# A hybrid decoder layer on one core: logits of head pairs as 64-row products in two-bank tiles, values projected 512 columns at once, q and k split once, stick products on GpSimd

## The chip, the cores and the metric

One of the eight cores of a Trainium2 chip runs the kernel. The metric is the device time of one execution in microseconds (us). The kernel before takes 709.08 us, the median of three runs (707.87 to 709.63).

## What is computed

One decoder layer and a final norm, for 512 tokens of width 1024, all in float32:

```python
h = h + W_o [ stick-breaking heads || differential heads ](RMSNorm(h) W_in)
h = h + W_down( gelu(g) * u ),  [g, u] = causal_dwconv3( RMSNorm(h) W_up )
h = h + sigmoid(RMSNorm(h) W_pg) * (p W_pp)
```

Eight stick-breaking heads of dimension 64 weigh token s for token t by beta_ts times the product of (1 - beta_tj) over s < j < t, where beta is the sigmoid of the scaled logits and s < t. Four differential heads have two maps of dimension 64 each: the weights are softmax(Q1 K1' + b1) - lambda softmax(Q2 K2' + b2), the values are 128 wide, and each head's output is normalized. The FFN is 2816 wide.

## The kernel before

All matrix products keep float32 accuracy by splitting each operand into a high and a low part of a reduced type (float32r); `mm3` then makes three products: high x high, low x high, high x low. `split_w` makes the parts of a weight, 128x1024 at a time: the cast of the high part on ScalarE (ACT), the subtraction for the low part on VectorE (DVE).

**The stages.** x is loaded, transposed and scaled into `xg` (eight tiles, hidden dimension on partitions). `proj_qk` projects q and k of a pair of heads (128 columns each, 24 products of 512 columns each for q and for k). There are eight such pairs: four of stick heads and four of the two maps of a differential head. `proj_v` projects values, 256 columns at a time, in four calls of 96 products. `sb_logits` and `sb_attn` do a stick pair: logits in five banks with the causal mask added by a product, two sigmoids on ACT, a scan on DVE for the running product of (1 - beta), a multiplication by beta on DVE (line L418), transposes on TensorE (PE), the split of the weights (L432, L433), the weighted sums. `diff_probs` does a differential head's logits and softmax, by blocks of 128 tokens: a reduction from PSUM on DVE (L479), an exponential on ACT (L483), the two maps combined (L488, L489). `diff_out` does the transposes (L503), the split, the weighted sums, and the norm: squares on ACT, their sums on PE (L516), a power on GpSimd (POOL, L106), and a broadcast on PE (`bcast_row`, L116). The output projection comes in two halves: the first sums over the stick heads (mix tiles 0 to 3), the second over the differential heads (mix 4 to 7) and feeds `residual`, whose squares POOL adds up (L539). The FFN starts from about 264 us.

**The operands of the logits.** The contraction is only 64 deep, so `proj_qk` stacks the high and the low part of q on the 128 partitions (`st`), and holds the high part of k on both halves (`dh`) and the low part on both halves (`dl`): two products of 128 rows give all four terms for one head. The copy into the other half is made by POOL (L341), 32 copies of 64x512.

**PSUM** has eight banks: pool `psA` has two one-bank tiles `mm` for projections and six one-bank tiles `z` for all else. `slot` gives the work tiles, 128x512 each.

**What sets the order.** The program is written in one sequence; a scheduler then orders each engine's instructions by its own estimate of when they can start and by priorities. Within an engine the order is then fixed and each instruction waits for what it needs. The table `fill` puts weight loads and projections of later pairs beside a stick pair's attention. The second value projection stands in pair 1, the third in pair 3, the fourth among the differential heads. After the attention the same PSUM pool goes on, as a ring of all eight tiles:

```python
ring = itertools.cycle([psm, psm, psz, psz, psz, psz, psz, psz])
self.psm = lambda: next(ring)()
```

Of the kernel before, what the change touches and what calls it, by code (L numbers as in the profile page):

```python
# [35 lines left out]
SLOTS = {"w": 7, "h": 6, "l": 6, "strip": 2, "qkt": 2, "o": 2}  # L36
# [4 lines left out]
class Kern:  # L41
# [24 lines left out]
    def slot(self, s, tag="w"):  # L66
        return self.work.tile([P, T], F32, tag=tag, name=self.nm(s), bufs=SLOTS[tag])

# [242 lines left out]
    def proj_qk(self, sp, stacked):  # L311

# [4 lines left out]
        halves = [slice(0, HD), slice(HD, P)]  # L317
        for i in range(2):
# [7 lines left out]
            if i == stacked:  # L326
                st = self.qk.tile([P, 2, T], F32R, tag="st", name=self.nm("st"))
                for h in range(2):
                    nc.scalar.copy(st[halves[h], h, :], t[halves[h], :])
                    nc.vector.tensor_sub(st[halves[1 - h], h, :], t[halves[h], :], st[halves[h], h, :].bitcast(F32))  # L330
                res.append(st)
            else:
                dh = self.qk.tile([P, 2, T], F32R, tag="dh", name=self.nm("dh"))
                dl = self.qk.tile([P, 2, T], F32R, tag="dl", name=self.nm("dl"))
                for h in range(2):
                    o = halves[h]
                    nc.scalar.copy(dh[o, h, :], t[o, :])  # L337
                    nc.vector.tensor_sub(dl[o, h, :], t[o, :], dh[o, h, :].bitcast(F32))  # L338
# [3 lines left out]
                res.append((dh, dl))  # L342
        return res

    def prep_v(self, off):
        raw = self.load_w([(0, self.a["w_in"][0][:, off : off + 2 * P])], KT, 2 * P)
        return [self.split_w(raw[:, i * 4 : (i + 1) * 4, :]) for i in range(2)]

    def proj_v(self, sp, stacked):

        nc = self.nc
        v = self.vp.tile([P, NB, 4 * P], F32R, tag="v", name=self.nm("v"))
        for tb in range(NB):
            ps = self.psv()
            for k in range(KT):
                xs = tuple(x[:, tb * P : (tb + 1) * P] for x in self.xg[k])
                self.mm3(ps[:, : 2 * P], xs, tuple(x[:, k % 4, :] for x in sp[k // 4]), k == 0, k == KT - 1)
            r = self.rstd1[:, tb : tb + 1]
            if stacked:
                oh, ol = (v[:, tb, :].rearrange("p (h d) -> p h d", d=HD)[:, i::2, :] for i in range(2))  # L360
                pv = ps[:, : 2 * P].rearrange("p (h d) -> p h d", d=HD)
            else:
                oh, ol = v[:, tb, : 2 * P], v[:, tb, 2 * P :]
                pv = ps[:, : 2 * P]
# [6 lines left out]
    def sb_logits(self, q, k):  # L371
        nc = self.nc

        banks = [[(h, 3, 0)] for h in range(2)] + [[(h, 2, 0), (h, 0, 384)] for h in range(2)] + [[(0, 1, 0), (1, 1, 256)]]
        z = []
        for parts in banks:
            ps = self.psz()
            z.append(ps)
            first = True
            for h, tb, col in parts:  # L380
                n = (tb + 1) * P
                for x in range(2):
                    nc.tensor.matmul(
                        ps[:, col : col + n], lhsT=q[:, h, tb * P : (tb + 1) * P], rhs=k[x][:, h, :n],
                        start=first, stop=False, skip_group_check=True,
                    )
                    first = False
# [444 lines left out]
```

## Time and profile before

| what | value |
|---|---|
| median of three runs | 709.08 us (707.87 to 709.63) |
| the profiled execution, its own time | 708.74 us |
| span of its trace | 707.0 us |
| TensorE (PE) busy | 681.5 us, 96% |
| VectorE (DVE) busy | 465.4 us, 66% |
| ScalarE (ACT) busy | 333.3 us, 47% |
| GpSimd (POOL) busy | 93.0 us, 13% |

The profile is that of one execution. Busy time is that of instructions that compute; a product's time in it is longer than the place it takes, since products overlap, so how fast products follow each other is read from their starts. The granted clock is TensorE's, as a share of full speed. The releaser of a wait is the instruction that ended it. Time outside of the span is 1.7 us.

### The profile page before, as it was taken

The numbers are of one execution on the slowest core, as the hardware profiler recorded it, in microseconds if no ns is written. First come the engines' busy times: TensorE is split into PE (matmuls) and PEld (weight loads), VectorE is DVE, ScalarE is ACT, GpSimd is POOL, SyncE is SP. The second block draws the span as 40 slices with busy tenths as digits, with TensorE's granted clock in tenths as the row PEclk, the third lists the DMA queues.
The fourth block names the chain that finished last, engine by engine and source line by source line (L and its number), as shares of the span: only waits on it lengthen the run. The fifth ranks groups of instructions, "written<-read, shape, count | busy, mean of one in ns | idle before, by whom it ended". The sixth has DMA issues, their size and how long they took to land. (4 is left out here: it accounts for less than half of the span.)

```text
span 707.0 us, 8645 instructions
## 1 busy us (share of the span) xinstructions
PE 681.5 (96%) x3363; PEld 573.0 (81%) x3363; DVE 465.4 (66%) x719; ACT 333.3 (47%) x535; POOL 93.0 (13%) x84
## 2 busy tenths in 40 slices
PE   6998999899999998999999999999999999999995
PEld 5887888788988876888888888888888878888885
DVE  6777979978686648597777777677734241516444
ACT  5555655667674435455444444444423131417422
POOL 2233034304221006000000000000000010102001
PEclk9999999999999999999999999999999999999998
DMA  8763231142351103333322233321423222327002
GB/s 270 245 244 94 60 109 44 28 119 90 90 208 62 60 0 98 91 110 120 119 74 87 79 120 119 100 79 59 131 93 105 66 98 90 104 62 265 1 28 92
DMA packets 69840, 72.72 MB, mean 103 GB/s; under 512 B 2357, under 2 KB 60926, under 8 KB 69799
## 3 DMA queue, kind: packets, MB, share of 16 engines
q1 hardware_dynamic: 66464, 65.80, 29.1%
q10 hardware_dynamic: 2695, 4.27, 1.6%
q0 software_dynamic: 640, 2.10, 0.7%
q8 instruction: 26, 0.43, 0.3%
q14 instruction: 15, 0.12, 0.1%
HBM read 67.95 MB, written 6.84 MB: 106 GB/s over the span
## 5 line engine op out<-in xcount | busy, mean ns | idle before, releaser
L99 DVE TENSOR_TENSOR wlo<-wraw,whi 128x1024 fp32r<-128x1024 f32 (+1 forms) x104 | 127.6, 1229 | 87.2 <-ACT whi L98 86.0
L98 ACT CAST whi<-wraw 128x1024 fp32r<-128x1024 f32 (+1 forms) x104 | 107.4, 1034 | 148.8 <-PE z L80 85.7
L539 POOL TENSOR_TENSOR sqacc<-sqacc,sq 128x512 f32<-128x512 f32 x14 | 22.4, 1603 | 364.2 <-issue 259.1
L79 PE MATMUL mm<-xgh,whi 128*128 128x512 f32 x128 | 50.5, 395 | 1.4 <-ACT whi L98 1.4
L80 PE MATMUL mm<-xgl,whi 128*128 128x512 f32 x128 | 50.3, 394 | 0.0
L81 PE MATMUL mm<-xgh,wlo 128*128 128x512 f32 x128 | 50.2, 392 | 0.0
L341 POOL TENSOR_SCALAR dh<-dh 64x512 fp32r<-64x512 f32 x16 | 28.2, 1759 | 115.2 <-ACT dh L337 103.8
L691 DVE TENSOR_TENSOR vpad<-z,rb 128x512 f32<-128x512 f32 x34 | 23.2, 687 | 26.8 <-PE z L81 26.7
L693 ACT ACTIVATE y<-vpad,par,par 128x512 f32<-128x512 f32 x44 | 35.7, 814 | 3.2 <-DVE vpad L691 3.0
L79 PE MATMUL mm<-whi,xgh 128*128 128x256 f32 x96 | 28.7, 299 | 6.0 <-DVE v L367 5.9
L695 DVE SCALAR_TENSOR_TENSOR y<-vpad,par,y 128x512 f32<-128x512 f32 x44 | 32.9, 751 | 1.3
L694 DVE SCALAR_TENSOR_TENSOR y<-vpad,par,y 128x512 f32<-128x512 f32 x44 | 32.7, 745 | 0.0
L697 ACT ACTIVATE y<-y 128x512 f32<-128x512 f32 x22 | 13.9, 630 | 34.9 <-DVE y L695 34.8
L79 PEld LDWEIGHTS mm<-xgh,whi 128*128 128x128 f32 x128 | 24.2, 189 | 6.4 <-ACT whi L98 1.8
L80 PE MATMUL mm<-wlo,xgh 128*128 128x256 f32 x96 | 28.6, 298 | 0.0
L81 PE MATMUL mm<-whi,xgl 128*128 128x256 f32 x96 | 28.6, 298 | 0.0
L81 PEld LDWEIGHTS mm<-xgh,wlo 128*128 128x128 f32 x128 | 24.1, 188 | 4.8
L80 PEld LDWEIGHTS mm<-xgl,whi 128*128 128x128 f32 x128 | 24.2, 189 | 4.5
L417 DVE TENSOR_TENSOR_SCAN cum<-cum,fresh 128x512 f32<-128x512 f32 x20 | 25.2, 1270 | 1.4 <-ACT cum L408 1.1
L79 PEld LDWEIGHTS mm<-whi,xgh 128*128 128x128 f32 x96 | 19.5, 203 | 6.9 <-DVE v L367 6.3
L341 POOL TENSOR_SCALAR dl<-dl 64x512 fp32r<-64x512 f32 x16 | 24.9, 1558 | 1.5 <-DVE dl L338 0.3
L483 ACT ACTIVATE pr<-pr,nmx 128x512 f32<-128x512 f32 (+3 forms) x32 | 17.7, 556 | 10.9 <-DVE nmx L479 10.7
(673 smaller groups left out, 1925.0 us busy)
## 6 DMA issues: line engine op xcount, KB each, us to landing
wraw<-in_w_up SPq DMA_DIRECT2D x22, 1024.0 KB, 5.1
wraw<-in_w_in SPq DMA_DIRECT2D x16, 512.0 KB, 7.1
wraw<-in_w_down SPq DMA_DIRECT2D x8, 1024.0 KB, 4.9
wraw<-in_w_in SPq DMA_DIRECT2D x5, 1024.0 KB, 5.1
wraw<-in_w_o SPq DMA_DIRECT2D x4, 1024.0 KB, 5.0
wraw<-in_w_ple_gate SPq DMA_DIRECT2D x4, 1024.0 KB, 5.7
wraw<-in_w_down SPq DMA_DIRECT2D x4, 768.0 KB, 4.2
sk<-sk ACTq DMA_DIRECT2D x1, 2560.0 KB
```

Source lines behind the costliest of these rows:

```text
L79: nc.tensor.matmul(ps, lhsT=l[0], rhs=r[0], start=start, stop=False, **kw)
L80: nc.tensor.matmul(ps, lhsT=l[0], rhs=r[1], start=False, stop=False, **kw)
L81: nc.tensor.matmul(ps, lhsT=l[1], rhs=r[0], start=False, stop=stop, **kw)
L98: nc.scalar.copy(hi, raw)
L99: nc.vector.tensor_sub(lo, raw, hi.bitcast(F32))
L341: nc.gpsimd.tensor_scalar(x[halves[1 - h], h, :], x[halves[h], h, :].bitcast(F32), 1.0, None, op0=ALU.mult)
L417: nc.vector.tensor_tensor_scan(back, back, fresh, 1.0, op0=ALU.mult, op1=ALU.max)
L539: nc.gpsimd.tensor_add(sqacc, sqacc, sq)
L691: nc.vector.tensor_mul(u[:, 2 : T + 2], ps, rb2)
L693: nc.scalar.activation(y, u[:, 2 : T + 2], AF.Identity, scale=self.cw(2, ch), bias=self.g("cb", ch))
L694: nc.vector.scalar_tensor_tensor(y, u[:, 1 : T + 1], self.cw(1, ch), y, op0=ALU.mult, op1=ALU.add)
L695: nc.vector.scalar_tensor_tensor(y, u[:, 0:T], self.cw(0, ch), y, op0=ALU.mult, op1=ALU.add)
```

## The change

- `psA` has three two-bank tiles `z` in place of six of one bank, and the work tiles of `slot` are two banks wide and half as many.
- `proj_qk` splits q and k once, 128x512 each: high part by ACT, low part by DVE. Nothing is stacked or copied to another half.
- `logits`, new, serves both kinds of heads. A pair's two heads lie on partitions 0 to 63 and 64 to 127. For each block of 128 tokens three products of 64 rows (high x low, low x high, high x high) are made for each head, the two heads by turns, each into its own bank of a two-bank tile: 24 products a pair, where there were 16 of 128 rows.
- `proj_v` projects 512 columns in one call of 96 products into four banks: the stick values ahead of pair 0, the differential ones after head 0's logits.
- `sb_attn` works on three two-bank tiles: sigmoids up to 1024 wide, scans 512 wide, the multiplication by beta on GpSimd, up to 1024 wide. `diff_out` evicts 1024 and 256 columns in place of four pieces.
- `fill` is gone. `psA` is closed after the attention, and the second half of the output projection and all that follows uses a new pool of eight one-bank tiles.

```diff
-SLOTS = {"w": 7, "h": 6, "l": 6, "strip": 2, "qkt": 2, "o": 2}
+SLOTS = {"w": 4, "h": 3, "l": 3, "strip": 2, "qkt": 2, "o": 2}
+WIDE = ("w", "h", "l")
...
+        shape = [P, 2, T] if tag in WIDE else [P, T]
+        return self.work.tile(shape, F32, tag=tag, name=self.nm(s), bufs=SLOTS[tag])
...
-                for x in (dh, dl):
+            o = self.qk.tile([P, 2, T], F32R, tag=tag, name=self.nm(tag))
+            nc.scalar.copy(o[:, 0, :], t)
+            nc.vector.tensor_sub(o[:, 1, :], t, o[:, 0, :].bitcast(F32))
+            res.append(o)
+        return res
+
+    def logits(self, q, k):
...
+        z = [self.psz() for _ in range(3)]
+        where = {3: (0, 0), 2: (1, 0), 0: (1, 3 * P), 1: (2, 0)}
+        with self.tc.high_priority(2000):
+            for tb in (3, 2, 0, 1):
+                b, col = where[tb]
+                n = (tb + 1) * P
+                for i, (x, y) in enumerate(((0, 1), (1, 0), (0, 0))):
                     for h in range(2):
-                        nc.gpsimd.tensor_scalar(x[halves[1 - h], h, :], x[halves[h], h, :].bitcast(F32), 1.0, None, op0=ALU.mult)
...
+                        o = slice(h * HD, (h + 1) * HD)
+                        nc.tensor.matmul(
+                            z[b][:, h, col : col + n], lhsT=q[o, x, tb * P : (tb + 1) * P], rhs=k[o, y, :n],
+                            start=i == 0 and tb != 0, stop=i == 2 and tb != 2, skip_group_check=True,
+                        )
+        return z, where
+
+    def proj_v(self, off, stacked):
...
+        v = self.vp.tile([P, NB, 2 * T], F32R, tag="v", name=self.nm("v"))
+        pss = [z[:, i, :] for z in (self.psz(), self.psz()) for i in range(2)]
+        for k0 in range(0, KT, 4):
+            raw = self.load_w([(0, self.a["w_in"][0][k0 * P : (k0 + 4) * P, off : off + T])], 4, T)
+            for i in range(2):
+                wh, wl = self.split_w(raw[:, 2 * i : 2 * i + 2, :])
+                for tb in range(NB):
+                    for j in range(2):
+                        k = k0 + 2 * i + j
+                        xs = tuple(x[:, tb * P : (tb + 1) * P] for x in self.xg[k])
+                        self.mm3(pss[tb], xs, (wh[:, j, :], wl[:, j, :]), k == 0, k == KT - 1)
...
-            nc.vector.tensor_mul(beta, beta, c[:, 1 : T + 1])
...
+            for c0 in range(off, 2 * T, T):
+                back = c[:, c0 : c0 + T][:, ::-1]
+                r0 = (3 - g) * P
+                fresh = self.fresh[:, r0 : r0 + T] if g else self.fresh[:, 0:1].to_broadcast([P, T])
+                nc.vector.tensor_tensor_scan(back, back, fresh, 1.0, op0=ALU.mult, op1=ALU.max)
+            nc.gpsimd.tensor_mul(beta, beta, c[:, off + 1 : 2 * T + 1])
...
-        self.psz = lambda: psA.tile([P, T], F32, tag="z", name=self.nm("z"), bufs=6)
+        self.psz = lambda: psA.tile([P, 2, T], F32, tag="z", name=self.nm("z"), bufs=3)
...
-        fill = {0: [(wv, mv, 0), (wq, mq, 1)], 1: [(wv, mv, 1), (wq, mq, 2)], 2: [(wq, mq, 3)], 3: [(wq, mq, 4), (wv, mv, 2)]}
-        mv(0)
+        v = self.proj_v(2 * SBW, True)
         for pair in range(4):
             lg = self.sb_logits(*qk[pair])
-            for w, _, i in fill[pair]:
-                w(i)
-            self.sb_attn(pair, lg, v[pair // 2])
...
+            wq(pair + 1)
+            self.sb_attn(pair, lg, v)
+            mq(pair + 1)
...
         pr[0] = self.diff_probs(0, *qk[4])
         mq(5)
         wq(6)
-        wv(3)
+        v = self.proj_v(5 * SBW, False)
...
-        mv(3)
...
         self.close("work", "vp", "qk")
-        psm, psz = self.psm, self.psz
-        ring = itertools.cycle([psm, psm, psz, psz, psz, psz, psz, psz])
-        self.psm = lambda: next(ring)()
+        self.close("psA")
+        psB = self.open("psB", space=PSUM)
+        self.psm = lambda: psB.tile([P, T], F32, tag="mm", name=self.nm("mm"), bufs=8)
```

**How the order moves: PE at stick pair 3.** Before, at the transposes of pair 3 (L430, from `beta`), with `mm` the projection of q of the second differential head:

```order
L79 MATMUL mm_1668<-xgh_148,whi_1585 128x512
L80 MATMUL mm_1668<-xgl_149,whi_1585 128x512
L430 MATMUL z_1334<-ident,beta_1329 128x128
L430 MATMUL z_1334<-ident,beta_1319 128x128
L430 MATMUL z_1334<-ident,beta_1309 128x128 x2
L430 MATMUL z_1343<-ident,beta_1329 128x128
L430 MATMUL z_1343<-ident,beta_1324 128x128
L430 MATMUL z_1343<-ident,beta_1314 128x128 x2
```

Behind the last transpose sixteen more products of that `mm` tile and five of the next follow before the first weighted sum (L442). Now, from the third logits tile of pair 3 (`z_1065`) over its masks (L386) to the transposes (L432, into `z_1124`):

```order
L445 MATMUL z_980<-awl_976,v_396 128x256
L445 MATMUL z_980<-awh_953,v_396 128x128
L445 MATMUL z_980<-awl_954,v_396 128x128
L346 MATMUL z_1065<-k_1060,q_1030 128x256 x6
L386 MATMUL z_1065<-maskR,identR 128x128 x2
L432 MATMUL z_1124<-ident,beta_1119 128x128
L432 MATMUL z_1124<-ident,beta_1113 128x128
L432 MATMUL z_1124<-ident,beta_1107 128x128 x2
```

No projection stands between the masks and the transposes any more; the nine products nearest to them (L81 to L83 into an `mm` tile) stand just ahead of the eight weighted sums of pair 2 that these rows end. Further on, head 0's last logits (`z_1265`) and then the wide value projection (`z_1402`):

```order
L445 MATMUL z_1160<-awl_1156,v_396 128x256
L445 MATMUL z_1160<-awh_1133,v_396 128x128
L445 MATMUL z_1160<-awl_1134,v_396 128x128
L346 MATMUL z_1265<-k_1240,q_1210 128x256 x6
L81 MATMUL z_1402<-whi_1406,xgh_123 128x512
L82 MATMUL z_1402<-wlo_1407,xgh_123 128x512
L83 MATMUL z_1402<-whi_1406,xgl_124 128x512
L81 MATMUL z_1402<-whi_1406,xgh_135 128x512
```

Before, the values of the first two differential heads were 256 columns wide, in `mm` tiles, and stood ahead of pair 3's transposes; now those of all four come behind head 0's logits.

**PE at the output projection and differential head 3.** Before, around head 3's logits (L477), with `mm_2614` and `mm_2628` of the first half (mix 0 to 3):

```order
L477 MATMUL z_2361<-dl_2295,st_2262 128x384
L477 MATMUL z_2372<-dh_2294,st_2262 128x256
L477 MATMUL z_2372<-dl_2295,st_2262 128x256
L80 MATMUL mm_2614<-mix3l,whi_2610 128x512
L81 MATMUL mm_2614<-mix3h,wlo_2611 128x512
L79 MATMUL mm_2628<-mix0h,whi_2610 128x512
L80 MATMUL mm_2628<-mix0l,whi_2610 128x512
L81 MATMUL mm_2628<-mix0h,wlo_2611 128x512
```

and some 60 rows later the second half (mix 4 and on) ahead of head 2's weighted sums (`z_2432`):

```order
L81 MATMUL mm_2660<-mix3h,wlo_2643 128x512
L79 MATMUL mm_2703<-mix4h,whi_2699 128x512
L80 MATMUL mm_2703<-mix4l,whi_2699 128x512
L81 MATMUL mm_2703<-mix4h,wlo_2700 128x512
L79 MATMUL mm_2703<-mix5h,whi_2699 128x512
L80 MATMUL mm_2703<-mix5l,whi_2699 128x512
L81 MATMUL mm_2703<-mix5h,wlo_2700 128x512
L79 MATMUL z_2432<-dwh_2404,v_2126 128x512
```

Now head 3's logits (L346, `z_1965` and `z_1966`) stand behind the last product of the first half (`mm_2270`, six rows above these) and inside head 1's weighted sums (`z_1831`):

```order
L81 MATMUL z_1831<-dwh_1820,v_1401 128x384
L82 MATMUL z_1831<-dwl_1821,v_1401 128x384
L83 MATMUL z_1831<-dwh_1820,v_1401 128x384
L81 MATMUL z_1831<-dwh_1827,v_1401 128x256
L346 MATMUL z_1965<-k_1928,q_1898 128x512 x6
L346 MATMUL z_1966<-k_1928,q_1898 128x384 x6
L346 MATMUL z_1966<-k_1928,q_1898 128x128 x6
L82 MATMUL z_1831<-dwl_1828,v_1401 128x256
```

and the second half's first product (`mm_2317`) behind the last broadcast (L118) of head 3's norm:

```order
L118 MATMUL z_2112<-identR,bch_2137 128x128
L118 MATMUL z_2112<-identR,bcl_2138 128x128
L81 MATMUL mm_2317<-mix4h,whi_2313 128x512
L82 MATMUL mm_2317<-mix4l,whi_2313 128x512
L83 MATMUL mm_2317<-mix4h,wlo_2314 128x512
L81 MATMUL mm_2317<-mix5h,whi_2313 128x512
L82 MATMUL mm_2317<-mix5l,whi_2313 128x512
L83 MATMUL mm_2317<-mix5h,wlo_2314 128x512
```

The rows between `z_1965` and `mm_2317` are the transposes, weighted sums, norms and logits of the differential heads; no row of the projection is among them.

## Rows read from the trace of the kernel before

**Rows 1.** The page, parts 1 and 2: busy time of the engines, granted TensorE clock.

```profile
PE 681.5 (96%) x3363; PEld 573.0 (81%) x3363; DVE 465.4 (66%) x719; ACT 333.3 (47%) x535; POOL 93.0 (13%) x84
...
PEclk9999999999999999999999999999999999999998
```

**Rows 2.** PE's waits: engine, line waited for, us in total, times, longest.

```profile
PE mm L79 <- DVE v L367: 5.9, 2, 3.3
```

**Rows 3.** Timeline of PE: start, us, instruction, idle before and its releaser.

```profile
59.13 0.28 PE L81 MATMUL mm<-whi,xgl 128*128 128x256 f32 x1
62.73 0.39 PE L79 MATMUL mm<-whi,xgh 128*128 128x256 f32 x1 [3.32 <-DVE v L367]
```

**Rows 4.** Stretches: length, busy us of PE, PEld, DVE, ACT, POOL, clock, DMA.

```profile
64.20:67.70 3.50, 3.50 (x19) 3.50 (x19) 0.00 (x0) 0.00 (x0) 0.00 (x0) 0.51 0.02 5
139.30:142.80 3.50, 3.50 (x19) 3.50 (x19) 1.78 (x3) 1.03 (x1) 0.00 (x0) 0.51 0.00 0
270.00:275.00 5.00, 3.67 (x16) 2.33 (x14) 5.00 (x5) 3.08 (x5) 3.97 (x4) 1.00 0.00 0
275.00:280.00 5.00, 3.75 (x16) 2.66 (x15) 5.00 (x5) 1.24 (x2) 2.60 (x2) 1.00 0.01 3
```

**Rows 5.** Timeline of PE, differential head 3.

```profile
222.43 0.48 PE L477 MATMUL z<-dh,st 128*128 128x512 f32 x1
222.74 0.39 PE L477 MATMUL z<-dl,st 128*128 128x512 f32 x1
222.97 0.39 PE L477 MATMUL z<-dh,st 128*128 128x512 f32 x1
...
224.13 0.28 PE L477 MATMUL z<-dh,st 128*128 128x256 f32 x1
224.25 0.28 PE L477 MATMUL z<-dl,st 128*128 128x256 f32 x1
...
241.38 1.29 PE L503 MATMUL z<-ident,pr 128*128 128x128 f32 x10
243.34 0.49 PE L79 MATMUL z<-dwh,v 128*128 128x512 f32 x1 [0.67 <-ACT dwh L505]
...
254.53 0.27 PE L116 MATMUL z<-identR,bcl 128*128 128x128 f32 x1
```

**Rows 6.** Groups of DVE, ACT, POOL to 300 us: count, busy us, mean ns, idle before.

```profile
L99 DVE TENSOR_TENSOR wlo<-wraw,whi 128x1024 fp32r<-128x1024 f32 x41 | 52.6, 1288 | 17.5 <-ACT whi L98 17.3
L417 DVE TENSOR_TENSOR_SCAN cum<-cum,fresh 128x512 f32<-128x512 f32 x20 | 25.2, 1270 | 1.4 <-ACT cum L408 1.1
L338 DVE TENSOR_TENSOR dl<-qkt,dh 64x512 fp32r<-64x512 f32 x16 | 13.0, 813 | 0.2
L479 DVE CUSTOM_DVE_ANT_0 pr<-z,strip 128x512 f32<-128x512 f32 x8 | 5.4, 690 | 0.9 <-PE z L477 0.8
L489 DVE SCALAR_TENSOR_TENSOR pr<-pr,rsm,pr 128x512 f32<-128x512 f32 x4 | 3.0, 748 | 0.5 <-ACT pr L488 0.5
...
L98 ACT CAST whi<-wraw 128x1024 fp32r<-128x1024 f32 x41 | 42.8, 1046 | 42.1 <-PE mm L80 13.3 <-PE z L80 8.1 <-DMA wraw<-in_w_in 7.1
L337 ACT CAST dh<-qkt 64x512 fp32r<-64x512 f32 x16 | 9.9, 616 | 2.6 <-DVE qkt L325 2.4
L483 ACT ACTIVATION_READ_ACCUMULATOR pr<-pr,nmx 128x1 f32 x32 | 6.0, 188 | 0.0
L483 ACT ACTIVATE pr<-pr,nmx 128x512 f32<-128x512 f32 x8 | 5.7, 719 | 10.3 <-DVE nmx L479 10.3
L538 ACT ACTIVATE sq<-hT 128x512 f32<-128x512 f32 x7 | 4.2, 618 | 0.3 <-POOL sqacc L539 0.3
...
L341 POOL TENSOR_SCALAR dh<-dh 64x512 fp32r<-64x512 f32 x16 | 28.2, 1759 | 115.2 <-ACT dh L337 103.8 <-issue 10.7
L539 POOL TENSOR_TENSOR sqacc<-sqacc,sq 128x512 f32<-128x512 f32 x7 | 11.3, 1620 | 17.9 <-ACT sq L538 17.6
L106 POOL TENSOR_TENSOR rcd<-nrv,mhalf 128x4 f32<-128x4 f32 x4 | 4.1, 1023 | 46.2 <-DVE nrv L105 31.8 <-PE z L477 14.4
```

More of the change, by code (lines that the diff above doesn't have):

```diff
@@ L309, in prep_qk, with proj_qk @@
         return [self.split_w(raw[:, :, i * P : (i + 1) * P]) for i in range(2)]
-    def proj_qk(self, sp, stacked):
+    def proj_qk(self, sp):
         nc = self.nc
         res = []
-        halves = [slice(0, HD), slice(HD, P)]
-        for i in range(2):
+        for i, tag in enumerate("qk"):
             wh, wl = sp[i]
@@ L353, in proj_v @@
         for tb in range(NB):
[L354 to L357, printed above, removed]
             r = self.rstd1[:, tb : tb + 1]
@@ L372, in sb_logits @@
         nc = self.nc
[L374 to L387, printed above, removed]
-            diag = [col // P + tb for _, tb, col in parts]
-            step = diag[1] - diag[0] if len(diag) == 2 else 1
-            nc.tensor.matmul(
-                ps.rearrange("p (a b) -> p a b", b=P)[:, diag[0] :: step, :], lhsT=self.identR,
-                rhs=self.maskR.unsqueeze(1).to_broadcast([P, len(diag), P]), start=False, stop=True, skip_group_check=True,
-            )
@@ L395, in sb_logits, with sb_attn @@
-        return banks, z
-    def sb_attn(self, pair, logits, v):
+        z, _ = self.logits(q, k)
+        for b, (d, nd) in enumerate(((3, 1), (2, 2), (1, 1))):
+            for h in range(2):
+                nc.tensor.matmul(
+                    z[b][:, h, :].rearrange("p (a b) -> p a b", b=P)[:, d : d + nd, :], lhsT=self.identR,
+                    rhs=self.maskR.unsqueeze(1).to_broadcast([P, nd, P]), start=False, stop=True, skip_group_check=True,
+                )
+        return z
+    def sb_attn(self, pair, z, v):
@@ L400, in sb_attn @@
         nc = self.nc
[L401 to L402 removed]
         at = {}
[L404 to L405 removed]
+        for g in range(3):
+            w = 2 * P if g == 2 else T
+            n = 2 * w
+            beta = self.slot("beta").rearrange("p a b -> p (a b)")[:, :n]
             c = self.cum[self.ncum % len(self.cum)]
             self.ncum += 1
[L408 to L420 removed]
@@ new lines, in sb_attn @@
+            nc.gpsimd.tensor_mul(beta, beta, c[:, off + 1 : 2 * T + 1])
+            for h in range(2):
+                b = beta[:, h * w : (h + 1) * w]
+                if g == 0:
+                    at[h, 3] = b
+                elif g == 1:
+                    at[h, 2], at[h, 0] = b[:, : 3 * P], b[:, 3 * P :]
+                else:
+                    at[h, 1] = b
+        tbanks = [[(h, 1, T * h + 0), (h, 3, T * h + 384)] for h in range(2)], [[(h, 0, T * h)] for h in range(2)], [[(0, 2, 0), (1, 2, 256)]]
@@ L423, in sb_attn @@
         where, w = {}, []
-        for b, parts in enumerate(tbanks):
-            ps = self.psz()
-            for h, s, col in parts:
+        for b, banks in enumerate(tbanks):
+            ps = self.psz().rearrange("p a b -> p (a b)")
+            n = T * len(banks)
+            for h, s, col in sum(banks, []):
                 where[h, s] = (b, col)
```

162 lines of the change are left out of this document (64 added, 98 removed).

## The prediction

> **What bounds the kernel now.** The page's first part comes first: TensorE (PE) is busy 96% of the span [rows 1], so nothing is won elsewhere unless PE waits for it, and a wait of PE is paid in full. The second view is PE's waits: the only large one is a value product that waits for the eviction of values on DVE, 5.9 us in two waits [rows 2]; the timeline shows one of them, from 59.13 to 62.73 [rows 3]. Third, the table by stretches: right after each of these waits 3.5 us run at a granted clock of 0.51, which is the 1.2 GHz level, and full speed comes back after that [rows 4]. In a stretch whose clock is half, 3.5 x 0.49 = 1.7 us are lost, twice, so 3.4. DVE at 66% is second [rows 1] and its queue is in order: what matters of DVE, ACT and GpSimd (POOL) is how long the chains through them are where PE has nothing else to do. The last view is the timeline of PE around differential head 3: from its first logits product at 222.43 to the last product that broadcasts its norm at 254.53 there are 32.1 us of chain [rows 5]. PE idles about 1 us in it (the longest wait is 0.67), because products of the output projection stand between the links. That is the place to look at in the new order.
>
> The sum is made against the profiled execution, 708.74 us (its span is 707.0); the median of the runs is 709.08, so the two agree within 0.05%. A change under 0.3%, about 2.1 us, can't be told from none.
>
> **What the change takes off PE.** A 512-column product comes every 0.23 us and a 256-column one every 0.12 [rows 5], so 0.45 ns a column. Logits: one pass over a head's four blocks is 1280 columns, 0.575 us. Before, a pair takes two passes for each of two heads, 2.30 us. Now each head takes three passes of 64 rows. If the two heads' products run at once on their two halves of the rows, a pair takes 3 passes, 1.73 us; if one after the other, 6, 3.45 us. Over eight pairs that is -4.6 or +9.2. No row shows two products at once: every row of the trace is spaced by its columns. I take the lower value, because what spaces products is columns streamed through rows, and these two share neither rows nor bank. Three of the eight sets (stick pair 3, heads 0 and 3) lie in stretches where PE will wait anyway, so five eighths count: **-2.9**, other end +5.8. Values: 384 products of 256 columns, 46.1 us, become 192 of 512, 44.2: **-1.9**. The two waits of values go, since the wide values are done before pair 0 and no narrow values follow: **-5.9**, and with them the two slow stretches: **-3.4**.
>
> The Trainium skill, "TensorE: Matmul & The Clock Gate", Part 3, states that small products on distinct row groups run concurrently, with starts some 4 ns apart. No run here shows it; by it the term would be the -2.9, without it +5.8.
>
> **What costs nothing.** The split of q and k (ACT and DVE: two full-height parts in place of four half-height ones of 616 and 813 ns [rows 6]) and the 32 copies on POOL (16 of them are 28.2 us [rows 6]) are hidden now under PE's products. They shorten chains of pairs 0 to 2, which the products of the next pair's q and k cover anyway. Merged evictions save some fixed cost a piece, under the same cover. The stick product moves to POOL: 128x512 with two inputs takes 1.62 us there [rows 6]. The 1024-wide one has no row: 1.6 if width cost nothing, 3.2 if it goes by width; I take 3.2. In pairs 0 to 2 it hides. In pair 3 DVE's queue ends later than POOL's first two products, so only the narrow third one is on the path.
>
> **New wait 1: pair 3.** Before, the diff values and q/k of heads 0 and 1 filled PE here. Now the order has pair 3's last masks directly followed by its transposes, which wait for POOL's last product. From the first scan DVE has, in its order: four scans (1.27 each), a weight split (1.29), the add of the pair before (0.8), the lower parts of q and k (1.4 together), the scan of the third tile (1.27) [rows 6]: 9.8. Then the POOL product, 1.62, and about 0.4 of hand-overs: 11.8 us. PE has 2.1 us of products left when the first scan starts, so it waits 9.7. Behind the transposes the first weights need a 1024-wide cast (1.05) and subtract (1.29) [rows 6]: about 2.2 more in small waits. Then comes the wide value projection of the differential heads. Its second pair of banks is a tile that holds head 0's second logits tile, and DVE reaches that only after the round trip of block 3: two reductions (0.69), exponential (0.72 and its read, 0.2), reciprocal and scaling (some 0.3), the scaled copy (0.72), the combination (0.75), then four shorter reductions (1.7 by columns) [rows 6], 6.7 with hand-overs; PE has 2.3 of products: 4.4. Together **+16.3** (11 to 18).
>
> **New wait 2: head 3.** The tiles being two banks wide, head 3's logits stand behind all of the first half of the output projection, and the second half, which sits in a new pool, behind the last broadcast. So no filler is left between. From the end of the first half to the logits: a 1024-wide cast behind a weight split of the same size on ACT (1.05 each), then on DVE head 2's reductions, a residual add, a weight split and the wide subtract: about 6 (2 to 8). Then the chain of before, 32.1 [rows 5]. PE's own work in these 38.1: 22 transposes, 3 x 12 weighted sums, 18 logits products (together), 36 small products, 13.4 us. It waits 24.7, where it idled 1 before: **+23.7** (18 to 26).
>
> **New wait 3: into the FFN.** The sums of squares and the broadcast now stand ahead of the first w_up product. After the last w_o product: add 0.7, cast and square 0.7 + 0.6, the POOL sum 1.62, four small products 0.5, the power on POOL 1.02 [rows 6], casts and hand-overs 1.3: 6.5. Before, PE lost 2.6 between 270 and 280 [rows 4]. **+3.9** (1 to 5).
>
> **The clock.** The waits that halved the clock were of 3.3 and 2.6 us [rows 2, 3]. The new ones are as long or longer at pair 3, the values, head 3 and the FFN: four times 1.7, **+6.8** (0 to 10).
>
> Sum: -2.9 - 1.9 - 5.9 - 3.4 + 16.3 + 23.7 + 3.9 + 6.8 = +36.6, so 708.7 + 36.6 = **745 us**.
>
> **The rivals.** *The heads' products go one after the other.* For: no row shows an overlap. Against: nothing they need is shared. +8.7 on the sum: 754. Chance 0.17.
>
> *The array empties at each change between 64-row and full products.* The order has 19 runs of logits, 38 changes. A product lasts 0.39 us where its place is 0.23 [rows 5], so 0.16 at each; some 24 of the changes lie outside the waits: +3.8, 749. Chance 0.10. The Trainium skill, "TensorEngine Tiling (Array Packing)", Key Properties, says that changing the tiling mode drains the engine; no run here shows it yet.
>
> *The new waits are shorter*, because DVE and ACT have little else to do in them: 2 us in place of 6 ahead of head 3, 11 at pair 3, no slow clock beyond what PE waits for anyway, 1 in the FFN: 745 - 4 - 5.3 - 2.9 - 3 = 730. Chance 0.13.
>
> *Faster.* Only the first four terms count, 708.7 - 14.1 = 694.6, if PE still finds work at the two places, above all at head 3. For it: the kernel of before does the same chain with 1 us of idle time. Against it: the order leaves no product of either projection between the links. It decides at 12 us: with less new waiting in all the kernel is faster by over 0.3%. Chance 0.05. Within 0.3%: 0.02.
>
> **How the numbers follow.** The forecast has 0.53. The range 726 to 760 takes in the two dearer cases, the short waits, and their bounds: 745 less 4, 5.3, 6.8 and 2.9 is 726; 754 with the drains and a slower POOL is 760. It leaves out the last rival, no change and a little at both ends. Faster 0.05, same 0.02, slower 0.93.
>
> **What would show it.** In the new profile PE's waits should show transposes for a POOL product once, near 10 us, values for a reduction near 4, and a row of waits between the two halves of the output projection that sum to 20 to 26 with PE about one third busy there; PE's share near 90%; clock 0.5 after pair 3. Logits of two heads should start nearly together; a start spacing of 0.23 would give the first rival. A head-3 stretch with PE above 80% busy would make the forecast wrong, and so would pair 3's transposes within 4 us of its masks.

## The result and the profile after

| | before | after |
|---|---|---|
| median | 709.36 us (707.87 to 710.06, 4 runs) | 762.17 us (759.48 to 762.32, 4 runs) |
| span of the profiled execution | 707.0 us | 760.5 us |
| PE idle in it | 25.5 us | 57.5 us |
| mean granted clock | 0.992 | 0.952 |

The ratio is 1.0739, with a 95% interval of 1.0709 to 1.0768: the change costs 53 us. The forecast was 745, and its range ended at 760. The sign was right, the size was not. The page answers to [rows 1] with these two lines:

```profile
PE 703.0 (92%) x3239; PEld 574.2 (75%) x3239; DVE 448.5 (59%) x657; ACT 318.6 (42%) x477; POOL 65.4 (9%) x64
...
PEclk9999999968999558899999999999999999999998
```

PE has 124 products fewer and is busy 21.5 us longer. The second line says why a share of busy time misleads here: its digits, one for each 19 us, fall to 6 near 160 us and to 5 from 247 to 285, so that PE counts as busy while it works at part of its speed.

PE's waits answer to [rows 2] (engine, line waited for, us in total, times, longest):

```profile
PE z L432 <- POOL beta L413: 9.9, 1, 9.9
PE mm L551 <- POOL sqacc L545: 7.1, 2, 4.5
PE z L522 <- ACT dout L520: 4.8, 2, 2.9
PE z L81 <- DVE dwl L509: 4.5, 3, 2.4
PE z L118 <- DVE bch L114: 3.3, 2, 1.7
PE mm L81 <- ACT whi L100: 2.8, 2, 2.4
PE z L81 <- DVE nmx L480: 2.8, 1, 2.8
```

The two waits for values are gone. The largest is the one foreseen at pair 3's transposes. The lines with dwl, dout, bch and nmx are the links of the differential heads, each waiting for the one before it. The stretches with waits or a low clock, in rows of 20 us (length, busy us of PE, PEld, DVE, ACT, POOL, clock, DMA):

```profile
140.00:160.00 20.00, 10.12 (x66) 8.72 (x65) 14.59 (x13) 8.68 (x13) 6.63 (x3) 0.80 0.19 52
160.00:180.00 20.00, 16.20 (x77) 12.76 (x76) 11.74 (x35) 12.53 (x28) 0.00 (x0) 0.77 0.09 27
240.00:260.00 20.00, 12.60 (x64) 10.51 (x62) 10.29 (x36) 9.89 (x25) 1.01 (x1) 0.69 0.14 44
260.00:280.00 20.00, 13.79 (x60) 11.81 (x60) 9.61 (x32) 9.72 (x24) 1.01 (x1) 0.59 0.00 0
280.00:300.00 20.00, 17.06 (x63) 14.27 (x64) 7.55 (x12) 5.88 (x9) 2.42 (x5) 0.70 0.08 19
300.00:320.00 20.00, 13.97 (x60) 11.26 (x59) 15.30 (x18) 9.07 (x13) 9.24 (x7) 0.90 0.27 87
680.00:700.00 20.00, 17.02 (x74) 13.62 (x73) 11.72 (x15) 9.07 (x14) 4.67 (x3) 0.91 0.57 198
```

Such rows hold two losses: the length less PE's busy time is idle time, and busy time times (1 - clock) is what the clock takes. Summed from the same view in rows of 1 us, the clock took 3.4 us before and 23.8 after. So the 53.5 us between the spans divide into 32.0 of idle time, 20.4 of clock, and 1.1 left for the products themselves. The forecast had 38.0, 3.4 and -4.8: it was 6.0 over on idle time, 17.0 under on the clock and 5.9 under on the products, 16.9 under in all.

The low clock fills most of one long stretch and is not a short tail behind single waits. Head 3 in rows of 5 us:

```profile
255.00:260.00 5.00, 3.15 (x14) 2.88 (x14) 0.69 (x4) 0.00 (x0) 1.01 (x1) 0.50 0.00 2
260.00:265.00 5.00, 2.66 (x10) 1.86 (x10) 3.85 (x12) 3.06 (x8) 0.00 (x0) 0.50 0.00 0
265.00:270.00 5.00, 4.33 (x19) 3.71 (x20) 2.91 (x14) 4.01 (x14) 0.00 (x0) 0.69 0.00 0
270.00:275.00 5.00, 3.43 (x19) 3.06 (x18) 1.96 (x5) 1.43 (x3) 1.01 (x1) 0.65 0.00 0
275.00:280.00 5.00, 3.38 (x16) 3.19 (x14) 0.90 (x2) 1.22 (x2) 0.00 (x0) 0.50 0.00 0
280.00:285.00 5.00, 2.06 (x9) 1.98 (x9) 0.98 (x4) 0.69 (x1) 1.13 (x4) 0.50 0.01 2
285.00:290.00 5.00, 5.00 (x16) 4.32 (x17) 1.39 (x2) 0.62 (x1) 0.00 (x0) 0.50 0.01 3
```

The 1.2 GHz level is granted from 244.2 to 292.0 with two short breaks, at 251 and at 268. Each break comes after PE had run without a gap (from 245.33 and from 265.00, in weighted sums above all), and ends after it has waited again; the level is left for good after PE has run without a gap from 284.81. Nor is PE's share of the chain a third, as the prediction had it, but about two thirds: at half speed the same work fills twice the time. The timeline of PE there (start, us, instruction, idle before and its releaser):

```profile
240.77 0.48 PE L83 MATMUL mm<-mix3h,wlo 128*128 128x512 f32 x1
...
248.08 3.10 PE L346 MATMUL z<-k,q 64*128 64x512 f32 x18
...
272.89 0.80 PE L81 MATMUL z<-dwh,v 128*128 128x512 f32 x1 [1.57 <-DVE dwl L509]
...
276.47 0.41 PE L118 MATMUL z<-identR,bch 128*128 128x128 f32 x1
...
286.36 0.41 PE L118 MATMUL z<-identR,bcl 128*128 128x128 f32 x1
286.57 0.73 PE L81 MATMUL mm<-mix4h,whi 128*128 128x512 f32 x1
```

From the last product of the first half to head 3's logits are 7.3 us (about 6 were counted), and from there to the last broadcast 38.3, where [rows 5] gave 32.1. The twelve weighted sums from 272.89 to 276.47 take 3.6 us, where their 3 x 1280 columns at 0.45 ns come to 1.7; the broadcasts follow each other at 0.21 us.

The logits, at full clock, in pair 1 (a row may hold many products, here 18):

```profile
82.75 0.39 PE L81 MATMUL mm<-xgh,whi 128*128 128x512 f32 x1
83.06 1.77 PE L346 MATMUL z<-k,q 64*128 64x512 f32 x18
84.76 0.50 PE L445 MATMUL z<-awl,v 128*128 128x512 f32 x1
```

These 18 products have 6144 columns together, 2.8 us one after the other. They are through in 1.70: the two heads run at once. In the records the second head's product mostly starts 3 or 4 ns after the first's. The first rival is false. The Trainium skill, "TensorE: Matmul & The Clock Gate", Part 3, is borne out on this point. But a run has ends: the projection ahead of it holds its place 0.31 us (82.75 to 83.06) where others hold 0.23; the first pair of 512 columns takes 0.333 where the next takes 0.232; the last pair of the run, of 128 columns, takes 0.201 where the one before it takes 0.107. These three excesses, 0.09, 0.10 and 0.09 by the records, make some 0.28 us a run; there are 19 runs, and 16 of them show the first excess at 0.09 or 0.10. With a run of 6 (0.556 us) a pair costs 1.70 + 0.56 + 0.18 = 2.43; before, the eight pairs' logits took 20.35 us by their start spacings, 2.54 a pair. That 2.43 is the price of unbroken runs: all eight pairs, shorter runs included, take 18.6 us by their spacings at full clock, and with the first excess of 19 runs (1.7) 20.3, so that nothing is gained on the whole.

Pair 3 on DVE, then on POOL:

```profile
145.01 6.33 DVE L412 TENSOR_TENSOR_SCAN cum<-cum,fresh 128x512 f32<-128x512 f32 x4 [0.37 <-ACT cum L405]
...
153.21 1.65 DVE L328 TENSOR_TENSOR q<-qkt,q 128x512 fp32r<-128x512 f32 x1
154.78 0.68 DVE L328 TENSOR_TENSOR k<-qkt,k 128x512 fp32r<-128x512 f32 x1
155.38 1.21 DVE L412 TENSOR_TENSOR_SCAN cum<-cum,fresh 128x512 f32<-128x512 f32 x1
```

```profile
147.52 2.74 POOL L413 TENSOR_TENSOR beta<-beta,cum 128x1024 f32<-128x1024 f32 x1 [16.19 <-DVE cum L412]
151.50 2.80 POOL L413 TENSOR_TENSOR beta<-beta,cum 128x1024 f32<-128x1024 f32 x1 [1.25 <-ACT beta L406]
156.76 1.09 POOL L413 TENSOR_TENSOR beta<-beta,cum 128x512 f32<-128x512 f32 x1 [2.46 <-DVE cum L412]
```

This is the path that was forecast: four scans, a weight split, the lower parts of q and k, the last scan, POOL's narrow product. But the row of four scans is 6.33 long, not 4 x 1.21, and the lower part of q takes 1.65 where that of k takes 0.68. All scans in one row, by line (durations in ns, least, median, longest, then first and last start):

```profile
L412 DVE TENSOR_TENSOR_SCAN cum<-cum,fresh x20: 1197/1214/2961, 59.3 to 155.4; 128x512 f32<-128x512 f32 x20
```

It is not that each scan slows: one of the four, the last, takes 2.96, while POOL makes its first product. By the records three of the twenty take that long, one each in pairs 1 to 3. POOL's wide products are longer there too: two of the eight took 2.00, as this one in pair 1, the others 2.74 to 2.81.

```profile
94.23 2.00 POOL L413 TENSOR_TENSOR beta<-beta,cum 128x1024 f32<-128x1024 f32 x1 [1.25 <-PE z L386]
```

### The profile page after: what moved, and what is told of

It is laid out like the page before. It is cut to its first block, busy times and chain, and to the rows that moved or that the text cites. A ratio compares the mean times of both kernels' runs of the same rounds, so it can differ in the third digit from the quotient of the medians.

```text
span 760.5 us, 8216 instructions
## 1 busy us (share of the span) xinstructions
PE 703.0 (92%) x3239; PEld 574.2 (75%) x3239; DVE 448.5 (59%) x657; ACT 318.6 (42%) x477; POOL 65.4 (9%) x64
## 5 line engine op out<-in xcount | busy, mean ns | idle before, releaser
L100 ACT CAST whi<-wraw 128x1024 fp32r<-128x1024 f32 (+1 forms) x102 | 105.7, 1036 | 175.6 <-PE mm L82 141.8
L81 PE MATMUL mm<-xgh,whi 128*128 128x512 f32 x128 | 51.1, 402 | 4.4 <-ACT whi L100 2.8
L692 DVE TENSOR_TENSOR vpad<-mm,rb 128x512 f32<-128x512 f32 x44 | 30.3, 689 | 41.6 <-PE mm L83 41.6
L83 PE MATMUL mm<-xgh,wlo 128*128 128x512 f32 x128 | 50.8, 397 | 0.0
L413 POOL TENSOR_TENSOR beta<-beta,cum 128x1024 f32<-128x1024 f32 (+1 forms) x12 | 27.0, 2255 | 101.0 <-DVE cum L412 98.5
L81 PEld LDWEIGHTS mm<-xgh,whi 128*128 128x128 f32 x128 | 24.1, 190 | 11.4 <-ACT whi L100 3.5
L698 ACT ACTIVATE y<-y 128x512 f32<-128x512 f32 x22 | 13.9, 632 | 41.0 <-DVE y L696 41.0
L412 DVE TENSOR_TENSOR_SCAN cum<-cum,fresh 128x512 f32<-128x512 f32 x20 | 28.5, 1472 | 2.2 <-ACT cum L405 2.2
L81 PE MATMUL z<-whi,xgh 128*128 128x512 f32 x64 | 26.2, 412 | 2.8 <-DVE nmx L480 2.8
L83 PEld LDWEIGHTS mm<-xgh,wlo 128*128 128x128 f32 x128 | 24.3, 190 | 4.9
L83 PE MATMUL z<-whi,xgl 128*128 128x512 f32 x64 | 26.2, 409 | 0.0
L82 PE MATMUL z<-wlo,xgh 128*128 128x512 f32 x64 | 25.9, 405 | 0.0
L535 DVE TENSOR_TENSOR hT<-mm,hT 128x512 f32<-128x512 f32 x16 | 11.0, 687 | 18.8 <-PE mm L83 18.8
L346 PE MATMUL z<-k,q 64*128 64x512 f32 (+3 forms) x192 | 21.3, 351 | 0.8 <-DVE awl L435 0.8
L346 PEld LDWEIGHTS z<-k,q 64*128 64x128 f32 x192 | 16.2, 198 | 6.8 <-issue 3.9
```

Source lines behind the costliest of these rows:

```text
L81: nc.tensor.matmul(ps, lhsT=l[0], rhs=r[0], start=start, stop=False, **kw)
L82: nc.tensor.matmul(ps, lhsT=l[0], rhs=r[1], start=False, stop=False, **kw)
L83: nc.tensor.matmul(ps, lhsT=l[1], rhs=r[0], start=False, stop=stop, **kw)
L100: nc.scalar.copy(hi, raw)
L346: nc.tensor.matmul(z[b][:, h, col : col + n], lhsT=q[o, x, tb * P : (tb + 1) * P], rhs=k[o, y, :n], start=i == 0 and tb != 0, stop=i == 2 ...
L412: nc.vector.tensor_tensor_scan(back, back, fresh, 1.0, op0=ALU.mult, op1=ALU.max)
```

## The experiments

Each is one execution with its profile, where no number of runs is given. The kernel before, run again with them, had medians of 707.36, 708.46 and 709.74, with single runs from 705.2 to 711.9; a difference of 1 or 2 us between single executions is no more than that spread.

**e1_ring: fillers back at head 3.** The changed kernel, with `psA` kept:

```diff
-        self.close("psA")
-        psB = self.open("psB", space=PSUM)
-        self.psm = lambda: psB.tile([P, T], F32, tag="mm", name=self.nm("mm"), bufs=8)
+        psm, pair_half = self.psm, []
...
+        ring = itertools.cycle([psm, psm, psh2, psh2, psh2, psh2, psh2, psh2])
+        self.psm = lambda: next(ring)()
```

> The changed kernel, but the second half of the output projection goes on in the tiles of psA (a ring of the two mm tiles and the six halves of the z tiles) instead of a new pool behind it. Theory A (the waits at differential head 3 are there because no product of the projection may stand between the links): about 60 of the 96 products move into the waits, TensorE's idle time from 240 to 300 us falls from 16.5 us to under 10, the granted clock there rises from 0.66, and the time falls from 762 to 742 to 752. Theory B (the chain alone sets the end of the second half): the time stays within 3 us of 762.

751.78 us, 10.4 less, inside theory A's range. But only 36 products of the second half, not 60, now stand ahead of the last broadcast, and idle time from 240 to 300 falls to 13.0, not under 10. The chain is as long as in the changed kernel (38.2 us) but carries more work. By the sums over 1-us rows, as in all that follows, idle time falls from 57.5 to 51.7 and the clock's loss from 23.8 to 16.9, so a little more is won by the clock than by the waits. Its rows:

```profile
240.00:260.00 20.00, 13.25 (x81) 10.69 (x80) 11.31 (x37) 10.29 (x26) 1.01 (x1) 0.88 0.17 55
260.00:280.00 20.00, 16.83 (x76) 13.83 (x75) 9.06 (x30) 9.80 (x24) 1.01 (x1) 0.78 0.00 1
```

**e2_warm: the clock held up by idle work.**

```diff
+        for _ in range(8):
+            ps = self.psm()
+            for j in range(12):
+                nc.tensor.matmul(ps, lhsT=self.identR, rhs=self.mix[0][0], start=j == 0, stop=j == 11)
```

> The changed kernel with 96 extra products of 512 columns (a split of nothing: an identity by a finished tile, into the idle mm tiles; their results are not used), which come into the waits behind the first half of the output projection: 22 us more of TensorE work at full clock. Theory A (what was mis-sized is the clock: TensorE, only partly busy there, is held at the lower level, which lengthens its own part of the chain and the second half behind it): the clock from 245 to 300 us rises from 0.6 to over 0.9, and the time is 750 to 764 in spite of the added work. Theory B (the waits alone cost; the clock is a by-product): what does not fit in the waits is added, 768 to 776.

768.13 us, 6 more for 22 us of added products: the time is at the lower end of theory B's range, not in theory A's. Their order left none behind 270 us, and the clock shows just that:

```profile
240.00:260.00 20.00, 20.00 (x114) 16.56 (x113) 9.77 (x33) 9.91 (x25) 0.33 (x1) 1.00 0.13 45
260.00:280.00 20.00, 16.25 (x89) 13.29 (x89) 8.00 (x31) 8.41 (x22) 1.69 (x2) 0.97 0.00 1
280.00:300.00 20.00, 17.00 (x63) 14.75 (x64) 5.43 (x11) 2.80 (x6) 1.12 (x4) 0.60 0.00 1
```

Work that keeps PE filled raises the clock to 1.00, on the same chain. But the added products also stood in the way of the links (the chain took 41.0 us), so as a price of the clock the run is inconclusive.

**e8_warm_less: half of it, spread out.**

```diff
+            if hd >= 2 and b == 0:
+                self.late.append(hi[:, :T])
...
+        for rhs, n in [(self.mix[0][0], 2), (self.late[0], 1), (self.late[1], 1)]:
+            for _ in range(n):
+                ps = self.psm()
+                for j in range(12):
+                    nc.tensor.matmul(ps, lhsT=self.identR, rhs=rhs, start=j == 0, stop=j == 11)
```

> As e2, but only 48 extra products (11 us at full clock) whose results are not used: 24 behind the first half of the output projection, 12 that need head 2's first weights and 12 that need head 3's, so that they come at those heads' waits and not all at the start. Theory A (the lower clock lengthens TensorE's own links, so that work which keeps it up pays for part of itself): clock from 245 to 290 us over 0.8 and a time of 757 to 764. Theory B (the clock is a by-product of waiting and costs only what idle time would have covered): 766 to 772.

763.09 us, inside theory A's range: 11 us of added work cost about 1, at clocks of 0.89, 0.77 and 0.83 in the three 20-us rows from 240 on (0.69, 0.59 and 0.70 without it). One stretch stays under the 0.8 that was expected. The last part of the chain, from head 3's first weighted sum to the last broadcast, shows what the clock does to it:

```profile
276.91 0.40 PE L81 MATMUL z<-dwh,v 128*128 128x512 f32 x1
...
278.76 0.28 PE L118 MATMUL z<-identR,bch 128*128 128x128 f32 x1
...
287.55 0.41 PE L118 MATMUL z<-identR,bcl 128*128 128x128 f32 x1
```

With the sums and the broadcasts of head 2 at full clock it takes 10.6 us; in the changed kernel, all of it at the lower level, 13.5 (272.89 to 286.36). The chain as a whole is no shorter (38.1), since added products stand in it.

**e3_narrow_v: values as before.** The changed kernel, with values 256 columns wide and the table `fill` again:

```diff
-        v = self.proj_v(2 * SBW, True)
+        self.psv = self.psm
+        mv(0)
...
-        v = self.proj_v(5 * SBW, False)
+        wv(3)
```

> The changed kernel with the value projections of before: four of 256 columns in the one-bank tiles, at their old places in the program (the second beside pair 1, the third beside pair 3, the fourth among the differential heads). Theory A (pair 3's wait is there because the values no longer fill it): the 9.9 us wait of the transposes for the GpSimd product and the 2.8 us wait of the values vanish, and with them some 4 us of lower clock at 140 to 180 us; the time is 738 to 748, the waits at head 3 remain. Theory B (the chain of DVE and GpSimd sets pair 3): the 9.9 us wait remains and the time is within 4 us of 762.

749.35 us, 12.8 less. The wait at pair 3's transposes is gone; in its place values wait again for their eviction, as in [rows 2]:

```profile
PE mm L81 <- DVE v L374: 6.3, 3, 2.6
```

Idle time falls by 13.9 to 43.6; the clock's loss, 25.2, does not fall. It came out 1 us above what theory A gave. The 12.8 is a net sum: idle time and clock together take 14.8 us less at pair 3 and 9.1 less at head 3 (240 to 300), but 8.3 more up to 60 us.

**e6_narrow_v_ring: e1 and e3 together.**

```diff
-        v = self.proj_v(2 * SBW, True)
+        self.psv = self.psm
+        mv(0)
...
-        self.close("psA")
...
+        ring = itertools.cycle([psm, psm, psh2, psh2, psh2, psh2, psh2, psh2])
```

> The changed kernel with the edits of e1 and e3 together: narrow values at their old places, second half of the output projection in psA's tiles. What is left of the change: two-bank tiles, 64-row logits, single split, stick products on GpSimd, wide evictions. Theory A (the two losses stand in different stretches and add: 10.4 us and 12.8 us off 762): 735 to 742. Theory B (with filler back in both places the clock stays up as well, more than the sum): 722 to 734. Theory C (two-bank tiles alone hold the chain of the heads back, so the second edit gains little): above 744.

735.38 us, 26.8 less than the changed kernel where e1 and e3 alone gave 10.4 and 12.8. The edits add, with 3.6 to spare, and together they take back half of what the change costs. They do not part the two places cleanly, since e3 alone already takes some of the loss at head 3. What makes up the other half was not tested as a whole.

**e7_products_on_dve: the scans without POOL beside them.**

```diff
-            nc.gpsimd.tensor_mul(beta, beta, c[:, off + 1 : 2 * T + 1])
+            nc.vector.tensor_mul(beta, beta, c[:, off + 1 : 2 * T + 1])
```

> The changed kernel with the stick products back on VectorE, 1024 wide. Theory A (pair 3's wait is set by VectorE's queue of four scans, a weight split, an add and the split of q and k, and the product on GpSimd is a small last link): the wait of pair 3's transposes stays at 8.5 to 11.5 us and is now for VectorE; time 759 to 768. Theory B (the products on GpSimd, or the port they share with VectorE, which made the scans 1.47 us in place of 1.27, make the wait): it falls below 6 us, time under 757.

767.35 us, 5.2 more, of which the clock's loss is 4.5 (28.3 against 23.8). Nearly all of that extra loss lies at the start, the FFN and the last norm, and not where the edit is. Its scans by line (least, median, longest), and its wait at pair 3:

```profile
L412 DVE TENSOR_TENSOR_SCAN cum<-cum,fresh x20: 1197/1212/1226, 61.1 to 155.9; 128x512 f32<-128x512 f32 x20
```

```profile
PE z L432 <- DVE beta L413: 10.3, 1, 10.3
```

Without POOL's products no scan takes over 1.23 us, where the longest took 2.96 with them: it is POOL that holds them up. The Trainium skill, "SBUF — State Buffer", section "SBUF: two separate sides", says that a DVE operation with two SBUF inputs and a GpSimd operation that reads SBUF exclude each other for a whole instruction; these rows agree, one operation held long and its neighbours not at all. Yet the wait is no shorter, since DVE then makes the products itself (1.23 each at 1024 columns, where POOL's took 2.00 to 2.81). For pair 3's wait the two places differ by 0.4 us; by e3, what puts the wait there is the missing filler.

**e4_logits_alone: one part of the change on the kernel before.** The single split and the 64-row products, in one-bank tiles, with values, `fill` and the output projection as before (10 runs):

```diff
-    def proj_qk(self, sp, stacked):
+    def proj_qk(self, sp):
...
+            self.passes(q, k, pss, tb, 0, True)
...
-                    nc.tensor.matmul(ps[:, :n], lhsT=q[:, j, tb * P : (tb + 1) * P], rhs=k[x][:, j, :n], start=x == 0, stop=x == 1)
```

> The kernel before with one part of the change alone: q and k split once, logits as three passes of 64 rows, the two heads by turns into two one-bank tiles. Values, pools, stick products and evictions as before. Theory A (the 64-row logits are sound: -4.6 us of products, 30 runs of them cost some 0.18 us each for both ends, +5; without the copies on GpSimd and the stacked parts DVE's queue is shorter, and the waits for the values go from 5.9 us to 3): 698 to 706. Theory B (the logits by themselves cost time, by the changes between 64-row and full products): 711 to 718.

706.32 us (705.75 to 707.20), ratio 0.9975 (0.9955 to 0.9995), 0.3 above theory A's range. Idle time fell from 25.5 to 18.9 us and the clock's loss from 3.4 to 0. The products themselves took 7 us more (685.1 against 678). Here the scheduler cut the logits into 30 runs, some of one head alone.

**e5_whole_runs: e4, with a pair's blocks kept together.**

```diff
-        for blocks in (((3, 0),), ((2, 0), (0, 384)), ((1, 0),)):
-            pss = [self.psz(), self.psz()]
-            for tb, col in blocks:
-                self.passes(q, k, pss, tb, col, False)
+        tiles = [[self.psz(), self.psz()] for _ in groups]
+        with self.tc.high_priority(2000):
+            for blocks, pss in zip(groups, tiles):
+                for tb, col in blocks:
+                    self.passes(q, k, pss, tb, col, False)
```

> As e4 (the kernel before with the 64-row logits alone), but a pair's logits are made of all its blocks at once at high priority, into six one-bank tiles: 19 runs in place of 30, and fewer products whose partner of the other head does not follow directly. Theory A (each run of 64-row products costs 0.28 us for its two ends, and a product without its partner its full time): TensorE's product time falls by 3 to 6 us against e4, the time is 699 to 704 with no new wait. Theory B (the 64-row products cost by themselves, not by their runs): within 1.5 us of e4's 706.3.

701.49 us (700.98 to 703.46, 6 runs), ratio 0.9904 (0.9873 to 0.9935): **faster than both kernels** (by 1% than the one before, the whole interval below 1). By the traces (e5's is that of its slowest execution), with 19 runs in place of 30 the products take 4.3 us less than in e4 (680.8 against 685.1), 0.39 a run; part of it is that more products have the other head's right behind them. They still take 2.7 more than in the kernel before: what makes e5 faster is idle time, 19.2 against 25.5, and the clock's loss, 1.5 against 3.4. And the values, still 256 wide, hardly wait:

```profile
PE mm L79 <- DVE v L362: 0.5, 1, 0.5
```

**e9_late_sum: the last norm's sums moved.** In the changed kernel the four small products (eight in the trace's rows) that sum `sqacc` for the last norm stand right behind the last transposes; before, they stood behind 24 products of the per-layer projection and waited for nothing. Timeline of PE, changed kernel, then the kernel before:

```profile
690.78 0.66 PE L729 MATMUL mm<-ident,hT 128*128 128x128 f32 x4 [0.35 <-DVE hT L535]
694.07 1.29 PE L551 MATMUL mm<-ones,sqacc 128*128 128x1 f32 x8 [2.63 <-POOL sqacc L545]
695.22 0.77 PE L81 MATMUL mm<-whi,pT 128*128 128x512 f32 x1
```

```profile
647.47 0.39 PE L81 MATMUL z<-whi,pT 128*128 128x512 f32 x1
647.70 0.95 PE L545 MATMUL mm<-ones,sqacc 128*128 128x1 f32 x8
```

```diff
-        self.rstd_cols(rstd3, sqacc)
...
         self.ple_proj(sps, pl)
+        self.rstd_cols(rstd3, sqacc)
```

> The changed kernel with one line moved: the four small products that sum sqacc for the last norm stand behind the 24 products of the per-layer projection (w_ple_proj) and no longer directly behind the last transposes. Theory A: in the changed kernel they wait 2.6 us for POOL's last sum there, and the clock that falls behind this wait costs 1.7 more; in the kernel before they stand behind these 24 products and wait for nothing. So both go: the wait of these products for POOL shrinks from 7.1 us in two to 4.5 in one, the clock loss between 680 and 700 us from 1.7 to below 0.5, and the time is 3 to 5 us under that of the changed kernel: 757 to 759.5. Theory B: the norm is needed soon after, so what they no longer wait for is lost at the first gate products instead: 761 to 763, and a wait of 2 us or more appears at the gate products.

757.18 us (755.74 to 759.35, 6 runs), 5.0 less; in the traces the place itself (from 680) loses 4.3 less. The clock between 680 and 700 is 1.00, and the wait is that of the FFN alone:

```profile
PE mm L551 <- POOL sqacc L545: 4.5, 1, 4.5
```

## Why the prediction was right and wrong

By place, idle time and clock together (sums over 1-us rows, less what the same place lost before):

| step | forecast | measured |
|---|---|---|
| old waits of values and their clock | -5.9 - 3.4 | -9.2 |
| wait 1, pair 3 (140 to 180), with two clock terms | 16.3 + 3.4 | 18.5 |
| wait 2, head 3 (240 to 300), with one | 23.7 + 1.7 | 30.5 |
| wait 3, into the FFN (300 to 340), with one | 3.9 + 1.7 | 5.7 |
| last norm (from 680) | none | 4.7 |
| start (to 60) | none | 1.8 |
| products | -2.9 - 1.9 | +1.1 |

About 0.4 us lies in smaller pieces. So by place three steps make up most of the 16.9 us that the forecast was short: products 5.9, head 3 5.1, the last norm 4.7.

**The waits were placed rightly and sized well.** At pair 3's transposes 9.7 was worked out and 9.9 came. That it is so near is in part luck: POOL's narrow product took 1.09 where 1.62 was counted and the weight split 1.19 where 1.29 was, while one of four scans took 1.7 more and the lower part of q 1.0 more, held up by POOL. The wide product's 3.2, from the end that goes by width, was too high (2.00 to 2.81), and it reached the path by what it held up. The values waited 2.8 where 4.4 was counted. The FFN's place is right to 0.1. e3 and e6 show the pair-3 wait to come from the order (values and fillers). At head 3, e1 shows that about a third of the loss (9.8 of 30.5), and 5.4 at the FFN behind it, come from the second half's new pool; what the two-bank tiles do to the rest was not tested by itself.

**The step that failed is the clock's:** "four times 1.7, +6.8 (0 to 10)". It took the tail behind one wait [rows 4] and counted waits. Measured are 23.8 us in the whole trace. In the chain of links that wait for one another PE ran at the 1.2 GHz level for some 41 of the 48 us from 244.2 to 292.0, and lost 14.8 us in this one place (240 to 300), where 1.7 was forecast. The error goes on into wait 2: the chain was taken over from [rows 5] at 32.1 us, where PE ran at full speed, and its own links are PE's. It measured 38.3. Two sets of weighted sums (1.9 and 1.7 more), head 3's logits (3.0 where 1.7 is usual), 24 broadcasts (0.10 more each) and two sets of norm sums (1.84 where 0.95 is usual) grew by some 9 us together, and the chain by 6.2, so that a part of them must have lain beside work of DVE and ACT. That the clock made the chain longer is shown for its last part, by e8 (10.6 us against 13.5); for the whole it is added up from the trace, and no run isolates it: in e1 and e8 the clock's loss between 240 and 300 falls to 8.5 and 7.9, yet the chain, with other work in it, stays at 38.2 and 38.1. The idle time is smaller than the 24.7 forecast (16.5 between 240 and 300), as slow links fill it. Idle time and clock so came to 30.5 at this place where the forecast had 25.4: much of the clock's loss was counted as waiting. e1, e2 and e8 show that the clock follows how filled PE is: 0.69 and 0.59 in the two rows from 240 on without more work between the links, 0.88 and 0.78 in e1, 0.89 and 0.77 in e8, 1.00 and 0.97 in e2.

**The logits' term, -2.9, was wrong, and the second rival's mechanism right.** That rival was set apart from the forecast, though both hold: two heads run at once, and the ends of each run cost. It was priced at 3.8 with 24 changes at 0.16, and some 0.14 a change (0.28 a run) was measured. Besides, of the three pairs of 128-column blocks only the first takes its 0.06, the second 0.107. A pair's logits so cost 2.43 us at best where 2.54 were paid before. Over five pairs that would be -0.5; over all eight, shorter runs included, nothing is gained (20.3 against 20.35), and e4, with more runs and some of one head alone, shows a loss. The Trainium skill, "TensorEngine Tiling (Array Packing)", Key Properties, says that such a change drains the engine; the runs here agree with it and give its price. The rest of the miss lies beside the logits: by start spacings at full clock, the masks take 1.0 us more than before (3.3), the stick heads' weighted sums 1.1 (11.3) and the transposes of the heads and of the last stage 2.0 (17.8), while the products of `mm3`, where the -1.9 for values belongs, take 1.3 less. How much of this is the ends of runs, and how much products that show their full length ahead of a wait, is not shown.

**The last norm was missed.** The prediction follows the order only as far as the FFN. The term was the same as wait 3 (sums ahead of products that could cover them); e9 gives it 4.3 us by its place in the trace, 5.0 by the medians.

**The removed waits did not need the wide values.** "The two waits of values go, since the wide values are done before pair 0" is true of the change, but with narrow values e4 and e5 lose most of them too (1.1 and 0.5 us are left), with less for DVE and POOL to do for q and k. So this gain needed none of the parts that cost. The single split is not enough by itself: e3 has it, with narrow values, and its values wait 6.3 us.

Where the start's 1.8 comes from stays open.

## What to carry to other kernels

Where a chain that waits link by link loses its fillers, price PE's own links in it at the 1.2 GHz level, and the clock for the whole stretch: here that was 14.8 us beside 16.5 of waiting, and a forecast that put nearly all of it down as waiting came out 5.1 short at this place. Two 64-row products at once paid here only in long unbroken runs; keep a pair's blocks together, count the runs, and take 0.28 us off for each. When a change moves the order, read it to the last stage, and take the part that gives (here the single split and 64-row logits with e5's whole runs, 1% faster, by less waiting and not by cheaper products) without the part that reorders.

## What the runs showed that was not expected

- PE stayed at the 1.2 GHz level for most of 255 to 285 us, while busy 41 to 87% of each 5-us row.
- A POOL product held a single DVE scan up from 1.21 to 2.96 us and left the next ones alone; POOL's 1024-wide product with two inputs took 2.00 twice and 2.74 to 2.81 beside held DVE operations, DVE's 1.23.
- The last 128-column pair of a run took 0.201 us where the one before it took 0.107, the first pair of 512 columns 0.333 where the next took 0.232.
- e5, with the same number of runs as the changed kernel, is faster than the kernel before although its products take 2.7 us more.
